# Routed rows split into bfloat16 parts during routing, and the branch for an expert's slots 65 to 96 put in front of its gate products

## The chip, the cores and the metric

The kernel runs on one core of a Trainium2 chip. The metric is device microseconds of one execution, as the median over runs. The engines are named as in the profile: PE (TensorE, matrix products; PEld is its weight load, which overlaps), DVE (VectorE), ACT (ScalarE), POOL (GpSimd) and SP, which here issues nearly all transfers. An engine name with a q (PEq, SPq) is that engine's instruction queue.

## The reference, cut to what matters

A sequence of 256 rows of width 1024 passes a mixer (a Fourier part and a gated delta rule in two directions, with a context of 256 rows ahead of it) and then a mixture of 32 experts, of which each row takes its best 4:

```python
def _moe(h, w_router, b_router, w_gate, b_gate, w_up, b_up, w_down, b_down):
    logits = (h @ w_router + b_router).astype(jnp.float32)
    top_v, top_i = lax.top_k(logits, TOP_K)          # 4 of 32
    gates = jax.nn.softmax(top_v, axis=-1)
    ...
        xb = h_pad[tok]
        a = jnp.minimum(xb @ w_gate[e] + b_gate[e], SWIGLU_LIMIT)
        u = jnp.clip(xb @ w_up[e] + b_up[e], -SWIGLU_LIMIT, SWIGLU_LIMIT)
        y = (a * jax.nn.sigmoid(SWIGLU_ALPHA * a) * (u + 1.0)) @ w_down[e] + b_down[e]
        return y * gate[:, None].astype(y.dtype)
```

Everything is float32. Each expert has three weights of 1024x1024, so the experts' weights are 384 MB, each byte of which is used once.

## The kernel before, in words

**First part.** The mixer and the routing stand in pieces that `ORDER` names (`X0`, `X1`: output projection, row norm, router logits and top 4 of rows 0 to 127 and of rows 128 to 255; `w`: the load of one more weight chunk of 1 MB). A scheduler may move instructions of these pieces.

**Chunks.** An expert is 12 chunks of 1 MB: 0 to 3 gate, 4 to 7 up, 8 to 11 down. They go through a ring of 18 places (`ROOMS`), in order; SP issues a chunk when the place's last reader, 18 chunks earlier, is done. 16 chunks are under way before the experts begin; `load_ahead` issues 12 per expert.

**Experts.** From there on the order on PE, ACT, DVE and SP is that of the code (`manual_schedule`). Each expert has 64 fixed slots (`MAIN`), and 32 more (65 to 96) behind a branch that is taken when its count of rows is over 64. On PE, per expert e: two bias rows (L1154), 16 gate products into `pg` (L1160), two bias rows and 16 up products into `pu`, the branch L1319 with `hidden32` (gather, gate and up products and transposes for slots 65 to 96), the gather of rows for a later expert (L1121, from the rows' three bfloat16 parts `h2s` by one-hot products), four transposes (L1179), for even e `add_rows` (L1238, slots back to rows) and for odd e `gates_turned` (L1149), 16 down products into `pd` (L1188), and the branch L1345 with `down32`. A branch that isn't taken is a jump over the instructions of its block. A float32 product counts as two passes with a weight load each in the trace, so 16 products are x32 there.

**First expert.** The rows `h2a` are made by DVE (L1050) after routing. Expert 0 gathers its rows in float32 (`gather32`, L1129), two blocks of 128 columns at a time, between its gate products. The split into `h2s` (`split_rows`: ACT L1272, L1276; DVE L1274, L1278) comes behind the up products, then the gather of expert 1's rows, then `down_bias` (the down bias of all experts times the rows' gates: L1285, L1292 on PE).

Of the kernel before, what the change touches and what calls it, by code (L numbers as in the profile page):

```python
# [21 lines left out]
T = 256  # L22
# [70 lines left out]
for _n, _w in (("c", 8), ("cc", 8), ("g1", 8), ("conv", 60), ("gout", 1), ("alog", 16), ("dtb", 16), ("br", 32)):  # L93
# [21 lines left out]
def body(ctx, tc, x, cx, sv, rows, cf, mk, w_mod, w_in, w_out, w_router, w_gate, b_gate, w_up, b_up,  # L115
# [827 lines left out]


    g2h = g2q = gatT = None

    def late_rows():
        nonlocal g2h, g2q, gatT
        late = natx[:, 2].rearrange("p a h d -> p (a h d)")
# [64 lines left out]
    def start_sums(a):  # L1014
        for g in range(2):
            nc.tensor.matmul(yacc[a][g], ident, xnat[:, a, 512 * g:512 * g + 512], start=True, stop=False,
                             skip_group_check=True)
        yield
# [9 lines left out]
             "Y0": start_sums(0), "Y1": start_sums(1)}  # L1028
# [33 lines left out]
    bdg = yz[:, 0]  # L1062
    nc.gpsimd.memset(bdg, 0.0)
    for g, hs in enumerate(halves):
        nc.scalar.dma_start(bdg[64 * g:64 * g + 32], b_down[:, 512 * g:512 * g + 512])
    strb = keep.tile([128, 128], BF, name="strb")
    nc.gpsimd.tensor_copy(strb, C("strict"))
    pr = bank("t", 3, 32)
    nc.tensor.matmul(pr[:, 0], strb, mkb[:, 0], start=True, stop=True)
    nc.tensor.matmul(pr[:, 1], onesb, mkb[:, 0], start=True, stop=False)  # L1070
    nc.tensor.matmul(pr[:, 1], strb, mkb[:, 1], start=False, stop=True)
    nc.tensor.matmul(pr[:, 2], onesb, mkb[:, 0], start=True, stop=False)
    nc.tensor.matmul(pr[:, 2], onesb, mkb[:, 1], start=False, stop=True)
    for a in range(2):
        nc.vector.scalar_tensor_tensor(rk[:, a], pr[:, a], 1.0, selm[:, a], op0=OP.add, op1=OP.mult)
    io1 = C("iota1")

# [7 lines left out]
    oh_ = [None, None]  # L1085
    oh_[0], oh_[1], oh32_, ohov2, gfr = carve("A", [128, 128, 128, 64, 256], 2)
    nc.scalar.dma_start(gfr[:4], rows[14:16].rearrange("a (b f) -> (a b) f", b=2))
    hT__ = carve("A", [512, 512], 2)
    *xg_, ha0, ha1, hao2 = carve("hT", [1024, 1024, 512, 512, 1024])
    hao, hso = hao2[:, :512], hao2[:, 512:]  # L1090
    hs_, hu_ = carve("vnc", [512, 512])
    *og_, ot0, ot1, ov_, ovg_, xov_, qr_ = carve("gm", [256, 256, 256, 256, 256, 256, 256, 8])
# [147 lines left out]
    oh32 = onehot(oh32_, 0, 1, 0, MAIN, F32)  # L1240
    xgs = {p: xg_[p % 2].rearrange("p (k s) -> p k s", k=8) for p in range(E // 2)}
    ots = [v.rearrange("p (a t) -> p a t", a=2) for v in (ot0, ot1)]
    ohs, ogs, vs = {}, {}, {}
    for a in range(2):
        lr = part("mm", 1960 + 32 * a, 32)
        nc.scalar.activation(lr, lg[:, a], AF.Exp, bias=top[a])
        sm = tail.tile([128, 1], F32, name="sm", bufs=2)
        nc.vector.scalar_tensor_tensor(gat[:, a], lr, 1.0, selm[:, a], op0=OP.mult, op1=OP.mult, accum_out=sm)
        nc.vector.reciprocal(sm, sm)
        nc.vector.tensor_scalar(gat[:, a], gat[:, a], sm, None, op0=OP.mult)  # L1250
    cnt = keep.tile([1, 33], I32, name="cnt")
    nc.vector.tensor_copy(cnt[:, :32], pr[0:1, 2])
    over = keep.tile([1, 33], F32, name="over")
    nc.vector.tensor_scalar(over[:, :32], pr[0:1, 2], -float(SLOTS), None, op0=OP.add)
    nc.vector.tensor_scalar(over[:, :EARLY], pr[0:1, 2, :EARLY], -float(MAIN), None, op0=OP.add)
    nc.vector.tensor_reduce(over[:, 32:], over[:, :32], AX.X, OP.max)
    nc.vector.tensor_scalar(cnt[:, 32:], over[:, 32:], 0.0, None, op0=OP.max)
    dump("rk", rk)
    dump("gat", gat)
    pctx.close()  # L1260
    if "stop" in dbg:
        return
    mps = ctx.enter_context(tc.tile_pool(name="mps", bufs=1, space=PSUM))

    engines = [ET.PE, ET.Activation, ET.DVE]

    def split_rows():

        rest = [xg_[1].rearrange("p (k q) -> p k q", k=8), hao2.rearrange("p (k q) -> p k q", k=8)]
        src = [h2a[:, a].rearrange("p (q k) -> p k q", k=8) for a in range(2)]  # L1270
        for a in range(2):
            nc.scalar.activation(h2s[:, 0, a], src[a], AF.Copy)  # L1272
        for a in range(2):
            nc.vector.tensor_tensor(rest[a], src[a], h2s[:, 0, a], OP.subtract)  # L1274
        for a in range(2):
            nc.scalar.activation(h2s[:, 1, a], rest[a], AF.Copy)  # L1276
        for a in range(2):
            nc.vector.tensor_tensor(h2s[:, 2, a], rest[a], h2s[:, 1, a], OP.subtract)  # L1278

    def down_bias():  # L1280
        nc.vector.scalar_tensor_tensor(bdg, bdg, 2.0, g2h, op0=OP.mult, op1=OP.mult)
        p = mps.tile([128, T], F32, name="m")
        for a in range(2):
            for hs in halves:
                nc.tensor.matmul(p[hs.start:hs.start + 32, 128 * a:128 * a + 128], gat[:, a], ident, start=True,  # L1285
                                 stop=True, tile_position=(0, hs.start))
        for hs in halves:
            q = slice(hs.start, hs.start + 32)
            nc.vector.tensor_copy(gatT[q], p[q])
        for a in range(2):  # L1290
# [3 lines left out]
        nc.gpsimd.memset(yz, 0.0)  # L1294

    with tc.manual_schedule(engines={ET.PE, ET.Activation, ET.DVE, ET.SP}):
        for e in range(E):
            pair, j = divmod(e, 2)
            w = weights_[e]
            xg = xgs[pair][:, :, MAIN * j:MAIN * j + MAIN]  # L1300
# [15 lines left out]
            if e == 0:  # L1316
                split_rows()
            if e >= EARLY:
                with tc.If(vs[e] > MAIN, preferred_fallthrough_block=False):  # L1319
                    hidden32(e, w)  # L1320
            load_ahead(8)
            up_part(pu_, a)
            if e == 0:
                gather(xgs[0][:, :, MAIN:], ohs[0][:, :, 1:], range(8))
            elif pair + 1 < E // 2:
                gather(xgs[pair + 1], ohs[pair + 1], range(4 * j, 4 * j + 4))
# [3 lines left out]
            if e == 0:  # L1330
                down_bias()
            elif j == 0:
                add_rows(ots[(pair - 1) % 2], yp)
            else:
                gates_turned(ogs[pair], ots[pair % 2])
# [6 lines left out]
            if e == 0:  # L1342
                gather(xgs[1], ohs[1], range(4))
# [13 lines left out]
    with tc.If(v > 0):  # L1357
        for e in range(E):
# [3 lines left out]
            def more(first):  # L1362
                with tc.If(v > first):
# [4 lines left out]
                    xg = xgs[0][:, :, :64]  # L1368
# [82 lines left out]
```

## Time and profile before

| | |
|---|---|
| median of 3 runs | 1321.13 us (1320.93 to 1324.38) |
| the profiled execution | 1323.06 us, its span 1321.0 us |
| PE busy | 1181.6 us, 89% of the span |
| DVE / ACT / POOL busy | 419.9 / 175.6 / 94.7 us |
| weights and other reads | 447.5 MB; 422 GB/s where the queue is never empty |

The profiled execution's own time is 2.06 us over its span. Busy shares are averages over stages; the mixer ends, and the first expert begins, near 332 us.

### The profile page before, as it was taken

What the parts mean: (1) busy time and instruction counts of PE and PEld (TensorE: products, weight loads), DVE (VectorE), ACT (ScalarE), POOL (GpSimd) and SP (SyncE); (2) the same over time, 40 slices, a digit from 0 to 9 for tenths busy, and PEclk for the clock granted to TensorE, in tenths of its full rate; (3) what the DMA queues carried; (4) which work ended last, traced back from release to release, by engine and by line L of the source; (5) the groups of instructions that cost most, each with busy time, mean ns of one, the idle gap of its engine ahead of it and who ended that gap; (6) DMA issues with size and microseconds to landing.
All of it is one profiled execution on the core that took longest, in us unless ns stands there. A gap on an engine that the chain in (4) does not pass through costs nothing. (4 is left out here: it accounts for less than half of the span.)

```text
span 1321.0 us, 17783 instructions
## 1 busy us (share of the span) xinstructions
PE 1181.6 (89%) x7337; PEld 551.8 (42%) x7337; DVE 419.9 (32%) x909; ACT 175.6 (13%) x324; POOL 94.7 (7%) x90
## 2 busy tenths in 40 slices
PE   6989998989898998999989997988898989998995
PEld 3767776755443333333333333323243333333332
DVE  2598887647421112221212121211212111211112
ACT  3265444111200000000000000000000000000001
POOL 1032337130000000000000000000000000000000
PEclk9999998989898999999999999999998989998998
DMA  9913345736659999799999999999999899999992
GB/s 329 314 46 117 113 147 162 293 129 260 252 202 425 413 421 423 290 422 422 423 420 421 423 422 421 422 422 423 421 423 424 359 421 418 422 421 422 422 421 92
DMA packets 96176, 450.56 MB, mean 341 GB/s; under 512 B 9236, under 2 KB 44440, under 8 KB 46888
## 3 DMA queue, kind: packets, MB, share of 16 engines
q1 hardware_dynamic: 95024, 446.79, 84.3%
q8 instruction: 105, 1.72, 0.5%
q10 hardware_dynamic: 1016, 1.80, 0.4%
q14 instruction: 31, 0.25, 0.1%
HBM read 447.51 MB, written 1.05 MB: 340 GB/s over the span
## 5 line engine op out<-in xcount | busy, mean ns | idle before, releaser
L1188 PE MATMUL pd<-w,scA 128*64 128x512 f32 x1024 | 229.5, 600 | 3.2 <-issue 1.3
L1160 PE MATMUL pu<-w,schT 128*64 128x512 f32 x1024 | 227.2, 593 | 4.2 <-DMA w<-in_w_up 4.1
L1160 PE MATMUL pg<-w,schT 128*64 128x512 f32 x1024 | 228.0, 596 | 0.8 <-DMA w<-in_w_gate 0.7
L1188 PEld LDWEIGHTS pd<-w,scA 128*64 128x64 f32 x1024 | 72.1, 138 | 149.6 <-issue 140.0
L1160 PEld LDWEIGHTS pu<-w,schT 128*64 128x64 f32 x1024 | 72.0, 137 | 148.3 <-issue 129.5
L1349 DVE TENSOR_TENSOR xnat<-pd,natx 64x512 f32<-64x512 f32 x64 | 44.1, 689 | 268.4 <-PE pd L1188 267.9
L1160 PEld LDWEIGHTS pg<-w,schT 128*64 128x64 f32 x1024 | 71.9, 137 | 133.0 <-issue 126.4
L1121 PE MATMUL m<-scA,h2s 128*128 128x128 bf16 (+2 forms) x864 | 56.3, 225 | 48.2 <-issue 26.8
L1167 ACT ACTIVATE scvnc<-schT 128x512 f32<-128x512 f32 x32 | 20.2, 630 | 577.0 <-DVE schT L1166 577.0
L1166 DVE TENSOR_SCALAR schT<-pg 128x512 f32<-128x512 f32 x32 | 22.1, 692 | 207.6 <-PE pg L1160 207.6
L1121 PEld LDWEIGHTS <-h2s 128*128 128x128 bf16 x864 | 50.2, 103 | 75.5 <-PEq L1319 41.6
L1238 PE MATMUL y<-xnat,scgm 128*128 128x512 f32 x144 | 70.3, 634 | 6.6 <-issue 3.4
L1172 DVE TENSOR_SCALAR scvnc<-pu 128x512 f32<-128x512 f32 x32 | 22.1, 692 | 151.9 <-PE pu L1160 151.6
L1414 POOL TENSOR_TENSOR schT<-scvnc,scA 128x512 f32<-128x512 f32 x1 | 1.3, 1288 | 944.0 <-ACT scvnc L1413 944.0
L1180 ACT ACTIVATE scA<-pg 128x512 f32<-128x512 f32 x32 | 19.1, 597 | 296.8 <-PE pg L1179 292.5
L504 PE MATMUL u<-hT,w 128*128 128x256 f32 x192 | 51.2, 400 | 0.0
L1238 PEld LDWEIGHTS y<-xnat,scgm 128*128 128x128 f32 x144 | 28.5, 209 | 37.6 <-issue 36.0
L1122 DVE COPY schT<-m 128x512 f32<-128x512 f32 x31 | 21.4, 692 | 67.7 <-PE m L1121 67.7
L504 PEld LDWEIGHTS u<-hT,w 128*128 128x128 f32 x192 | 34.2, 193 | 7.0 <-issue 2.9
L315 ACT ACTIVATE w<-w,cst 128x256 f32<-128x256 f32 x80 | 33.7, 501 | 14.1 <-DMA w<-in_w_mod 13.3
L316 POOL TENSOR_TENSOR w<-w 128x1024 f32<-128x1024 f32 x10 | 23.7, 2370 | 94.4 <-ACT w L315 78.7
L1168 DVE SCALAR_TENSOR_TENSOR scvnc<-scvnc,schT 128x512 f32<-128x512 f32 x32 | 22.2, 692 | 22.3 <-ACTq L1319 20.2
(358 smaller groups left out, 1103.8 us busy)
## 6 DMA issues: line engine op xcount, KB each, us to landing
w<-in_w_gate SPq DMA_DIRECT2D x128, 1024.0 KB, 19.8
w<-in_w_up SPq DMA_DIRECT2D x128, 1024.0 KB, 19.3
w<-in_w_down SPq DMA_DIRECT2D x128, 1024.0 KB, 19.8
w<-in_w_mod SPq DMA_DIRECT2D x24, 1024.0 KB, 10.8
w<-in_w_in SPq DMA_DIRECT2D x6, 1024.0 KB, 7.9
w<-in_w_out SPq DMA_DIRECT2D x4, 1024.0 KB, 6.4
wk<-in_w_in SPq DMA_DIRECT2D x2, 1024.0 KB, 12.3
wv<-in_w_in SPq DMA_DIRECT2D x2, 1024.0 KB, 12.2
```

Of the source, the lines that this page charges most:

```text
L315: nc.scalar.activation(w[:, k], w[:, k], AF.Copy, scale=sil[:, k, 0:1])
L316: nc.gpsimd.tensor_tensor(w[:, 0:4], w[:, 0:4], w[:, 4:8], OP.add)
L504: nc.tensor.matmul(p[:, c, :], w[c2][:, k, 128 * c:128 * c + 128], hT[:, k, 256 * n:256 * n + 256], start=(k == 0), stop=(k == 7))
L1121: nc.tensor.matmul(p[:, i], h2s[:, s, a, k], o[a], start=(s + a == 0), stop=(s + a == 3))
L1122: nc.vector.tensor_copy(dst[:, ks[0]:ks[-1] + 1], p)
L1160: nc.tensor.matmul(p[64 * g:64 * g + 64], xg[:, k], w[k // 2][:, k % 2, 512 * g:512 * g + 512], start=False, stop=(k == 7), skip_group_che ...
L1166: nc.vector.tensor_scalar(a, p, 7.0, None, op0=OP.min)
L1168: nc.vector.scalar_tensor_tensor(hs_, hs_, 1.0, a, op0=OP.add, op1=OP.mult)
L1172: nc.vector.tensor_scalar(hu_, p, 7.0, -7.0, op0=OP.min, op1=OP.max)
L1188: nc.tensor.matmul(p[64 * g:64 * g + 64], hT_[:, k, 64 * i:64 * i + 64], w[8 + 2 * i + k // 2][:, k % 2, 512 * g:512 * g + 512], start=(i ...
L1238: nc.tensor.matmul(yacc[a][g], ot[:, a, :], y[:, g, :], start=False, stop=False, skip_group_check=True)
L1349: nc.vector.tensor_tensor(yp[MAIN * j:MAIN * j + MAIN, g, :], p[hs], g2h[hs], OP.mult)
```

## The change

Four edits belong together. (1) Rows 0 to 127 are split into their bfloat16 parts in a new routing piece `S`; rows 128 to 255 right after their top 4 (ACT and DVE, in halves of 512 columns; POOL subtracts for rows 0 to 127). The first gather, `gather_first`, uses these parts: 48 bfloat16 products into one bank, then two copies. `split_rows` and `gather32` go. (2) The gates and counts that the later code needs (`gates_and_counts`) come behind expert 0's up products. (3) The branch with `hidden32` stands in front of an expert's gate products, no longer behind its up products. (4) `down_bias` comes in expert 3 instead of expert 0. Tiles move so that this fits (`qn`, `oh0_`, `bdg`).

```diff
+    def split_first():
+        ...
+        nc.vector.scalar_tensor_tensor(h2a[:, 0].rearrange("p (k q) -> p q k", k=8), nat_order(xgs[0]), st[:, 12:13],
+                                       nat_order(vec[:, 0]), op0=OP.mult, op1=OP.add)
+        rest = by_block(xgs[0])
+        nc.scalar.activation(h2s[:, 0, 0], by_block(h2a[:, 0]), AF.Copy)
+        nc.gpsimd.tensor_tensor(rest, by_block(h2a[:, 0]), h2s[:, 0, 0], OP.subtract)
+        nc.scalar.activation(h2s[:, 1, 0], rest, AF.Copy)
+        nc.gpsimd.tensor_tensor(h2s[:, 2, 0], rest, h2s[:, 1, 0], OP.subtract)
+    def gather_first(dst, oh):
+        p = mps.tile([128, 8, MAIN], F32, name="m")
+        for a in range(2):
+            for s in range(3):
+                for k in range(8):
+                    nc.tensor.matmul(p[:, k], h2s[:, s, a, k], oh[:, a, 0], start=(a + s + k == 0),
+                                     stop=(a + s == 3), skip_group_check=True)
+        for ks in (slice(0, 2), slice(2, 8)):
+            nc.vector.tensor_copy(dst[:, ks], p[:, ks])
...
+            if e >= EARLY:
+                with tc.If(vs[e] > MAIN, preferred_fallthrough_block=False):
+                    hidden32(e, w)
             pg_ = mps.tile([128, 512], F32, name="pg")
             bias_rows(e, pg_, bias[0])
             if e == 0:
-                for k in range(0, 8, 2):
-                    gather32(xg, oh32, k, ("m", "pd")[k // 2 % 2])
-                    if k >= 2:
-                        times(pg_, w[0:4], xg, (k - 2, k - 1))
-                ohs[0] = onehot(oh_[0], 0, 2, 0, MAIN)
-                times(pg_, w[0:4], xg, (6, 7))
-            else:
-                times(pg_, w[0:4], xg)
+                gather_first(xg, ohs[0])
+            times(pg_, w[0:4], xg)
...
             if e == 0:
-                split_rows()
-            if e >= EARLY:
-                with tc.If(vs[e] > MAIN, preferred_fallthrough_block=False):
-                    hidden32(e, w)
+                gates_and_counts()
...
-            if e == 0:
+            if e == 3:
                 down_bias()
```

Two places show how instructions move. The first is PE between the down products of one expert and the gate products of the next. Before, from the end of `down32` (L1238 is its `add_rows`) on, to the branch L1319:

```order
L1345 UNCONDITIONAL_BRANCH
L1154 LDWEIGHTS idb
L1154 MATMUL pg<-bgu,idb 64x512
L1154 LDWEIGHTS idb
L1154 MATMUL pg<-bgu,idb 64x512
L1160 MATMUL pg<-w,schT 64x512 x16
L1154 LDWEIGHTS idb
L1154 MATMUL pu<-bgu,idb 64x512
L1154 LDWEIGHTS idb
L1154 MATMUL pu<-bgu,idb 64x512
L1160 MATMUL pu<-w,schT 64x512 x16
L1319 COMPARE_AND_BRANCH
```

A full gate and up stage stands between the two branches. Now, from an expert's down products (L1185) on, where L1358 is the branch with `down32` (32 products L1224, four L1235) and L1321 the branch with the next expert's `hidden32`:

```order
L1185 MATMUL pd<-w,scA 64x512 x16
L1358 COMPARE_AND_BRANCH
L1358 UNCONDITIONAL_BRANCH
L1224 MATMUL m<-w,scgm 32x256 x32
L1235 MATMUL y_3010<-xnat,scgm 128x512
L1235 MATMUL y_3011<-xnat,scgm 128x512
L1235 MATMUL y_3012<-xnat,scgm 128x512
L1235 MATMUL y_3013<-xnat,scgm 128x512
L1358 UNCONDITIONAL_BRANCH
L1321 COMPARE_AND_BRANCH
L1321 UNCONDITIONAL_BRANCH
```

Where neither is taken, PE leaves the first block by a jump and lands on the next branch at once, with nothing between the two. The second place is DVE ahead of the first gate products. Before, between the top 4 of rows 128 to 255 and the first copies out of `gather32` (L1130):

```order
L1075 SCALAR_TENSOR_TENSOR rk<-t,mm 128x32 x2
L1110 TENSOR_TENSOR scA<-cfk,rk 128x64 x2
L1249 RECIPROCAL sm<-sm 128x1
L1252 CAST cnt<-t 1x32
L1250 TENSOR_SCALAR gat<-gat,sm 128x32
L1254 TENSOR_SCALAR over<-t 1x32
L1255 TENSOR_SCALAR over<-t 1x1
L1256 TENSOR_REDUCE over<-over 1x1
L1257 TENSOR_SCALAR cnt<-over 1x1
L1130 COPY schT<-m 128x2x64
```

Now the rows themselves (L1257), ranks, one-hots (L1104) and the two subtractions of the split stand there:

```order
L1257 SCALAR_TENSOR_TENSOR natx<-xg,st,vec 128x64x8 x2
L1261 SCALAR_TENSOR_TENSOR rk<-u,mm 128x32 x2
L1104 TENSOR_TENSOR scgm<-cfk,rk 128x128 x2
L1264 TENSOR_TENSOR vec<-natx,h2s 128x8x64 x2
L1267 TENSOR_TENSOR h2s<-vec,h2s 128x8x64 x2
L1268 CAST cnt<-u 1x32
L1269 TENSOR_SCALAR over<-u 1x32
L1270 TENSOR_SCALAR over<-u 1x1
L1127 COPY schT<-m 128x2x64
L1127 COPY schT<-m 128x6x64
```

The gates have left this place, and the split of rows 128 to 255 has come into it.

## Rows read from the trace of the kernel before

**Rows 1.** The page: DMA kinds, costliest groups (busy, mean ns, idle before, releaser)

```profile
q8 instruction: 105, 1.72, 0.5%
...
L1160 PE MATMUL pu<-w,schT 128*64 128x512 f32 x1024 | 227.2, 593 | 4.2 <-DMA w<-in_w_up 4.1
...
L1166 DVE TENSOR_SCALAR schT<-pg 128x512 f32<-128x512 f32 x32 | 22.1, 692 | 207.6 <-PE pg L1160 207.6
```

**Rows 2.** Stretches: us, PE, PEld, DVE, ACT, POOL busy, PEclk, DMA share, GB/s

```profile
380.00:390.00 10.00, 10.00 (x52) 3.28 (x50) 1.39 (x2) 0.63 (x1) 0.00 (x0) 1.00 0.29 120
...
540.00:550.00 10.00, 10.00 (x50) 3.36 (x48) 1.38 (x2) 0.63 (x1) 0.00 (x0) 1.00 0.34 143
...
570.00:580.00 10.00, 10.00 (x48) 3.04 (x44) 1.38 (x2) 0.63 (x1) 0.00 (x0) 1.00 1.01 422
```

**Rows 3.** Timeline of PE, experts 7 and 8: start, length, what [idle before]

```profile
565.67 0.41 PE L1154 MATMUL pg<-bgu,idb 96*64 96x512 bf16 x2 [0.55 <-PEq L1345]
...
591.29 0.41 PE L1154 MATMUL pg<-bgu,idb 96*64 96x512 bf16 x2 [0.64 <-PEq L1345]
...
619.25 0.41 PE L1154 MATMUL pg<-bgu,idb 96*64 96x512 bf16 x2 [0.45 <-PEq L1345]
```

**Rows 4.** Timeline of PE, expert 5, which takes both branches

```profile
504.90 1.36 PE L1121 MATMUL m<-scA,h2s 128*128 128x32 bf16 x48
...
506.99 7.05 PE L1207 MATMUL m<-w,scgm 128*32 128x512 f32 x64
...
529.22 3.66 PE L1227 MATMUL m<-w,scgm 128*32 128x256 f32 x64
```

**Rows 5.** Timeline of PE, waits of over 1 us ended by issue

```profile
417.62 0.72 PE L1121 MATMUL m<-scA,h2s 128*128 128x128 bf16 x10 [0.66 <-PEq L1319]
423.01 1.67 PE L1121 MATMUL m<-scA,h2s 128*128 128x128 bf16 x14 [4.67 <-issue]
...
665.29 0.47 PE L1121 MATMUL m<-scA,h2s 128*128 128x128 bf16 x4 [4.23 <-issue]
...
753.28 6.23 PE L1188 MATMUL pd<-w,scA 128*64 128x512 f32 x27 [1.30 <-issue]
...
809.37 1.97 PE L1121 MATMUL m<-scA,h2s 128*128 128x128 bf16 x17 [4.85 <-issue]
...
900.01 5.29 PE L1238 MATMUL y<-xnat,scgm 128*128 128x512 f32 x8 [3.44 <-issue]
...
958.76 2.51 PE L1121 MATMUL m<-scA,h2s 128*128 128x128 bf16 x24 [4.19 <-issue]
...
1069.76 0.91 PE L1121 MATMUL m<-scA,h2s 128*128 128x128 bf16 x7 [4.01 <-issue]
...
1209.28 1.65 PE L1121 MATMUL m<-scA,h2s 128*128 128x128 bf16 x14 [4.84 <-issue]
```

**Rows 6.** Timeline of PE, start and end of expert 2

```profile
402.60 0.41 PE L1154 MATMUL pg<-bgu,idb 96*64 96x512 bf16 x2 [0.64 <-PEq L1345]
...
437.10 0.41 PE L1154 MATMUL pg<-bgu,idb 96*64 96x512 bf16 x2 [0.55 <-PEq L1345]
```

**Rows 7.** A stretch behind the first of these waits, columns as in group 2

```profile
423.00:427.00 4.00, 3.99 (x21) 3.19 (x22) 1.09 (x3) 0.60 (x1) 0.00 (x0) 0.56 1.01 424
```

**Rows 8.** Timeline of PE behind the last expert, at the branch L1357

```profile
1308.40 1.09 PE L1404 MATMUL m<-scA,cfk 4*128 4x256 f32 x4 [1.66 <-PEq L1357]
```

**Rows 9.** Timeline of PE, expert 0 and what ends it

```profile
330.99 0.18 PE L1071 MATMUL t<-mkb,strb 128*128 128x32 bf16 x1 [2.55 <-DVE mkb L941]
...
362.92 1.07 PE L1285 MATMUL m<-cfk,gat 128*32 128x128 f32 x8
...
368.62 7.09 PE L1188 MATMUL pd<-w,scA 128*64 128x512 f32 x32
...
377.08 0.41 PE L1154 MATMUL pg<-bgu,idb 96*64 96x512 bf16 x2
```

**Rows 10.** Who waited for whom, SP's queue: us in total, times, longest

```profile
SPq L982 <- PEq L1319: 168.7, 21, 18.8
```

More of the change, by code (lines that the diff above doesn't have):

```diff
@@ L948, in late_rows @@
         nonlocal g2h, g2q, gatT
-        late = natx[:, 2].rearrange("p a h d -> p (a h d)")
+        late = qn.rearrange("p a h d -> p (a h d)")
         g2h, g2q, gatT = late[:, :512], late[:, 512:768], late[:, 768:]
@@ L1061, in body @@
     yp, yz = xnat[:, 0].rearrange("p (g f) -> p g f", g=2), xnat[:, 1].rearrange("p (g f) -> p g f", g=2)
[L1062 to L1065, printed above, removed]
     strb = keep.tile([128, 128], BF, name="strb")
     nc.gpsimd.tensor_copy(strb, C("strict"))
[L1068 to L1075, printed above, removed]
     io1 = C("iota1")
+    nc.gpsimd.memset(yz, 0.0)
     def carve(tag, widths, bufs=1):
@@ L1083, in carve @@
         return [t[:, int(i):int(j)] for i, j in zip(o, o[1:])]
[L1085 to L1092, printed above, removed]
+    *og_, ot0, ot1, ov_, ovg_, xov_, qr_, oh0_ = carve("gm", [256, 256, 256, 256, 256, 256, 256, 8, 128])
     ov = ov_.rearrange("p (k s) -> p k s", k=4)
@@ L1238, in add_rows @@
                 nc.tensor.matmul(yacc[a][g], ot[:, a, :], y[:, g, :], start=False, stop=False, skip_group_check=True)
-    oh32 = onehot(oh32_, 0, 1, 0, MAIN, F32)
-    xgs = {p: xg_[p % 2].rearrange("p (k s) -> p k s", k=8) for p in range(E // 2)}
-    ots = [v.rearrange("p (a t) -> p a t", a=2) for v in (ot0, ot1)]
     ohs, ogs, vs = {}, {}, {}
[L1244 to L1250, printed above, removed]
@@ L1259, in body @@
-    dump("gat", gat)
+    oh_ = [oh0_, None]
+    engines = [ET.PE, ET.Activation, ET.DVE]
+    hand = tc.manual_schedule(engines={ET.PE, ET.Activation, ET.DVE, ET.SP, ET.Pool})
+    with hand:
+        hv, rest = by_block(h2a[:, 1]), by_block(vec[:, 2])
+        hi, mid, lo = h2s[:, 0, 1], h2s[:, 1, 1], h2s[:, 2, 1]
+        kh = (slice(0, 64), slice(64, 128))
+        next(parts["X1"])
+        pr = bank("u", 3, 32)
+        nc.tensor.matmul(pr[:, 0], strb, mkb[:, 0], start=True, stop=True)
+        nc.tensor.matmul(pr[:, 1], onesb, mkb[:, 0], start=True, stop=False)
+        nc.tensor.matmul(pr[:, 1], strb, mkb[:, 1], start=False, stop=True)
+        nc.tensor.matmul(pr[:, 2], onesb, mkb[:, 0], start=True, stop=False)
+        nc.tensor.matmul(pr[:, 2], onesb, mkb[:, 1], start=False, stop=True)
+        for i in range(2):
+            fs = slice(512 * i, 512 * i + 512)
+            nc.vector.scalar_tensor_tensor(hv[:, :, kh[i]].rearrange("p k q -> p q k"), nat_order(xgs[1][:, fs]),
+                                           st[:, 13:14], nat_order(vec[:, 0, fs]), op0=OP.mult, op1=OP.add)
+            nc.scalar.activation(hi[:, :, kh[i]], hv[:, :, kh[i]], AF.Copy)
+        for a in range(2):
+            nc.vector.scalar_tensor_tensor(rk[:, a], pr[:, a], 1.0, selm[:, a], op0=OP.add, op1=OP.mult)
+        ohs[0] = onehot(oh_[0], 0, 2, 0, MAIN)
+        for q in kh:
+            nc.vector.tensor_tensor(rest[:, :, q], hv[:, :, q], hi[:, :, q], OP.subtract)
+            nc.scalar.activation(mid[:, :, q], rest[:, :, q], AF.Copy)
+        for q in kh:
+            nc.vector.tensor_tensor(lo[:, :, q], rest[:, :, q], mid[:, :, q], OP.subtract)
+        nc.vector.tensor_copy(cnt[:, :32], pr[0:1, 2])
+        nc.vector.tensor_scalar(over[:, :32], pr[0:1, 2], -float(SLOTS), None, op0=OP.add)
+        nc.vector.tensor_scalar(over[:, :EARLY], pr[0:1, 2, :EARLY], -float(MAIN), None, op0=OP.add)
@@ L1262, in body, with gates_and_counts @@
         return
+    oh_[1], ohov2, gfr = carve("A", [128, 64, 256], 2)
+    hT__ = carve("A", [512, 512], 2)
+    *xg_, ha0, ha1, hao2 = carve("hT", [1024, 1024, 512, 512, 1024])
+    hao, hso = hao2[:, :512], hao2[:, 512:]
+    hs_, hu_ = carve("vnc", [512, 512])
+    xgs_ = {p: xg_[p % 2].rearrange("p (k s) -> p k s", k=8) for p in range(E // 2)}
+    ots = [v.rearrange("p (a t) -> p a t", a=2) for v in (ot0, ot1)]
+    bdg = h2a[:, 0, :512]
     mps = ctx.enter_context(tc.tile_pool(name="mps", bufs=1, space=PSUM))
[L1265 to L1270, printed above, removed]
+    def gates_and_counts():
         for a in range(2):
[L1272 to L1278, printed above, removed]
+            lr = part("mm", 1960 + 32 * a, 32)
+            nc.scalar.activation(lr, lg[:, a], AF.Exp, bias=top[a])
+            sm = tail.tile([128, 1], F32, name="sm", bufs=2)
+            nc.vector.scalar_tensor_tensor(gat[:, a], lr, 1.0, selm[:, a], op0=OP.mult, op1=OP.mult, accum_out=sm)
+            nc.vector.reciprocal(sm, sm)
+            nc.vector.tensor_scalar(gat[:, a], gat[:, a], sm, None, op0=OP.mult)
+        nc.vector.tensor_reduce(over[:, 32:], over[:, :32], AX.X, OP.max)
+        nc.vector.tensor_scalar(cnt[:, 32:], over[:, 32:], 0.0, None, op0=OP.max)
+        nc.scalar.dma_start(gfr[:4], rows[14:16].rearrange("a (b f) -> (a b) f", b=2))
+        nc.gpsimd.memset(bdg, 0.0)
+        for g in range(2):
+            nc.gpsimd.dma_start(bdg[64 * g:64 * g + 32], b_down[:, 512 * g:512 * g + 512])
     def down_bias():
@@ L1293, in down_bias @@
                                  skip_group_check=True)
-        nc.gpsimd.memset(yz, 0.0)
-    with tc.manual_schedule(engines={ET.PE, ET.Activation, ET.DVE, ET.SP}):
+    with tc.manual_schedule(engines={ET.PE, ET.Activation, ET.DVE, ET.SP, ET.Pool}):
         for e in range(E):
@@ L1323, in body @@
             if e == 0:
-                gather(xgs[0][:, :, MAIN:], ohs[0][:, :, 1:], range(8))
+                gather(xgs_[0][:, :, MAIN:], ohs[0][:, :, 1:], range(8))
             elif pair + 1 < E // 2:
-                gather(xgs[pair + 1], ohs[pair + 1], range(4 * j, 4 * j + 4))
+                gather(xgs_[pair + 1], ohs[pair + 1], range(4 * j, 4 * j + 4))
             if e + 1 < E:
@@ L1329, in body @@
             hT_ = turned(a)
-            if e == 0:
+            if e == 3:
                 down_bias()
-            elif j == 0:
+            if j == 0 and e:
                 add_rows(ots[(pair - 1) % 2], yp)
-            else:
+            elif j:
                 gates_turned(ogs[pair], ots[pair % 2])
@@ L1342, in body @@
             if e == 0:
-                gather(xgs[1], ohs[1], range(4))
+                gather(xgs_[1], ohs[1], range(4))
             if e >= EARLY:
```

36 lines of the change are left out of this document (13 added, 23 removed), and 2 rows, old and new, of the table ORDER.

## Prediction

> **What bounds the kernel now.** I read the page first, then the stretches, then PE's timeline expert by expert. At 422 GB/s, a full stream, a chunk of 1 MB takes 1,048,576 / 422,000 = 2.49 us and an expert's 12 chunks 29.8 us [rows 2]. PE takes 25.6 us for an odd expert and 28.0 us for an even one, 26.8 us in the mean [rows 3]. So PE is the faster of the two in the steady state, and one would look for its waits in the weights. They are hardly there: the up products, the costliest of such groups, waited 4.1 us for weights in the whole execution [rows 1]. Instead the stream stands still at places, at 29% and 34% of its rate near 385 and 545 us, with PE busy all the while [rows 2]: the ring is full and PE is late. PE begins late (expert 0), loses about 20 us in each of the two experts that take their branches, and loses time in one more way, which I think decides this change.
>
> That way is seen in [rows 5]: seven times PE stands still for 3.44 to 4.85 us, and once for 1.30 us, "issue" (no semaphore, no data), each a few microseconds behind a branch L1319 that wasn't taken. Counted through the built order (a bfloat16 product is one load and one pass, a float32 one two of each), the seven are 5392, 3337, 2053, 1285, 2054 and 3338 instructions apart: 21.06, 13.04, 8.02, 5.02, 8.02 and 13.04 times 256. Instructions arrive in 105 packets, 1.72 MB, 16.4 KB each [rows 1], and PE's order to the end of the last expert is 104 times 256 long. So PE's instructions come in blocks of 256, and these are waits for a block. When do they occur? The jump over `hidden32` is 250 instructions long (of its 244 products and loads, 48 gather products and 64 passes in [rows 4], each with a load, are 224), so it nearly always lands in the next block. In all eight cases the block after that one begins 2 to 76 instructions behind the landing. In the other jumps over `hidden32` it begins 81 or more behind, and none waits. The jump over `down32` is 149 long (64 passes with loads [rows 4], and the adds). Where it stays within its block, the boundary has come as near as 7 instructions behind it, without a wait. I read this as: PE holds the block it is in and the next one; the one after is asked for on entry and comes some 5.4 us after the jump (417.62 to 423.01 [rows 5]).
>
> [...]
>
> **What each wait costs.** Expert 2 took 34.50 us [rows 6] for 27.96 [rows 3]: 6.5 us for a wait of 4.67. [...] The eight waits sum to 31.5 us, with seven times 1.9 us they cost 45 us.
>
> **The change part by part.**
>
> *The branch moved.* Now the jump over `down32` and that over the next expert's `hidden32` follow each other with one branch between. Together they are about 411 instructions, over a block and a half. Laid against the 256 grid that the seven waits fix (my count runs ahead of it by 2 per expert, taken out), this pair crosses two boundaries ahead of experts 2, 3, 8, 10, 11, 13, 15, 16, 18, 23, 24, 26, 28, 29 and 31, fifteen times (ahead of 5 and 21 too, but there the second branch is taken). [...] The wait is new in kind and not in the trace: from below, a jump to a far block with no stream running took 1.66 us at the end of the kernel [rows 8]; from above 5.4 us as in [rows 5]. The stream still runs, so I take a value near the upper row: wait and clock as measured for such a wait, 6.5 us each, 15 x 6.5 = 97 us. In experts 6, 9, 14, 19 and 27 one boundary is crossed and the next lies 10, 44, 30, 4 and 24 instructions behind the landing. There gate products run at 7.09 / 64 = 0.11 us per instruction (32 passes and 32 loads, as for the down products in [rows 9]), so 5.4 us less this way is 4.3, 0.6, 2.1, 5.0 and 2.8 us; with the clock about 20 us. The old eight vanish with their place: minus 45 us.
>
> The gap of 0.66 us between up products and gather [rows 5] goes; the transposes behind that gather wait for DVE's two steps of 0.69 us [rows 1] anyway, so 0.4 us of it counts. A second branch at the down products adds perhaps 0.2 us. Net minus 0.2 x 31 = 6 us; bounds 0 and minus 12.
>
> *Earlier release.* SP waited 168.7 us at the branch L1319 [rows 10], since `hidden32` was the last reader of gate and up chunks, taken or not. Now a gate place is free when the gate products are done. That lets the stream run further ahead; it gives PE only the 4 us that it waited. For the two experts that take the branch all eight chunks must be there before `hidden32`; the stream is then some 20 us ahead, so I cost it at nothing (without that lead, up to 10 us each).
>
> *The first expert.* From the ranks' products at 330.99 to expert 1's bias at 377.08 it takes 46.1 us [rows 9]. Now DVE has, behind the top 4 (about 330): two halves of the rows, ranks and one-hots (0.9 us), four halves of subtractions, at 0.69 us per half [rows 1] 5.0 us in all; ACT's halves and POOL's lie beside these. Eight products and a copy later the gate products begin, near 335.8. Then 7.1 gate, 7.1 up, 7.1 down [rows 9], two gathers of 48 and 24 products (1.9 and 1.5 us, an estimate from 10 products in 0.72 us [rows 5]), 1.4 for transposes and copy with nothing beside them, 0.6 branch: expert 1 begins near 362.5, 14.5 us earlier. `down_bias`, 362.92 to 368.62 = 5.7 us on PE [rows 9], comes back in expert 3, before the stream has caught up with PE, so moving it wins nothing. Net minus 8.5 us. Expert 1's chunks that wait for the gates' work (about 347) land by 357 and are needed from 370.
>
> *Sum*, against the profiled execution's own 1323.06 us: minus 8.5 (start), minus 4 (weights), minus 45 (old waits), minus 6 (gaps), plus 97 and 20 (new waits): 1376.6. That execution is 1.9 us above the median of its runs, so I predict 1374 us, 4% slower. With 3.5 to 7.3 us per wait it is 1330 to 1392.
>
> **The rivals.**
>
> *A jump pair costs no more than a jump.* Then PE's instructions are held further ahead than I read, or the fetch overlaps the drain. With waits as many as before the time is 1323 - 8.5 - 4 - 6 - 1.9 = 1303 us; with none at all the stream decides: filled from 347 us on, the last 366 chunks end at 347 + 366 x 2.49 = 1258, and with the last products and the final norm about 1280. For it: 62 branches stood in the kernel and only eight led to a wait. Against it: those eight stand on the grid, and no deeper store would let them arise. Chance 0.17.
>
> *Short fetches.* Once PE is slower than 29.8 us per expert, the ring is full, the stream has pauses and a block may come sooner, towards the 1.66 us of [rows 8]. It decides at one price: 15 waits and the 20 us scaled with them balance 8.5 + 4 + 45 + 6 = 63.5 us at 3.5 us per wait, clock included. At 3 us the time is about 1312. Against it: with 26.6 + 4 us per expert the stream still runs at 97%. Chance 0.13, of which 0.04 within 0.3%.
>
> *The change's own aim.* Start and earlier release shift the whole stream forward, and PE follows it. That needs PE to wait for weights now, which 4.1 us do not bear out; it is in the first rival's lower end.
>
> **How the numbers follow.** My forecast has 0.70. 0.3% (4 us) is about what a measurement of this kernel can tell from no change. Slower by more 0.70, within 0.04, faster 0.26 (0.17 and 0.09). The range reaches down to the first rival, 1300, and up to the upper bound, 1392; what it leaves out is the stream's 1280 and a dearer wait.
>
> **What would show it.** Right: waits of 3 us and more ended by PE's queue or issue at the fifteen places named, ahead of the bias rows, none behind the up products; the clock below full behind each; even and odd experts without a wait 0 to 0.4 us shorter; expert 1 near 362; SP's long waits at gate and up products and no longer at a branch; the stream never short. Wrong: gaps of 1 us or less at all pairs of branches, or PE waiting for weights over many experts.

## The result and the profile after

The changed kernel takes **1387.84 us** (median of 4 runs, 1386.80 to 1389.63) where the kernel before takes 1321.03 us on the same chip: a ratio of 1.0507 (95% interval 1.0478 to 1.0537), 5% slower. 1374 us, slower, was predicted, with a range of 1300 to 1392. The profiled execution took 1387.12 us, its span is 1385.0 us, 64.0 us more than before.

What PE waits for, from the view of the waits of the changed kernel (us in total, times, longest; L1151 are the bias rows, L1157 the gate and up products, L1321 the branch with `hidden32`):

```profile
PE pg L1151 <- issue: 76.4, 15, 6.5
PE pg L1151 <- PEq L1321: 14.3, 14, 1.2
PE pg L1157 <- issue: 13.7, 5, 4.6
```

Fifteen waits ended by issue stand ahead of an expert's first bias row, and five inside the gate products. Before there were eight, of 31.5 us together, behind the up products [rows 5]. Four of the fifteen and one of the five, from PE's timeline (experts 2, 3, 11, 31; the third row is expert 6):

```profile
398.27 0.64 PE L1151 MATMUL pg<-bgu,idb 96*64 96x512 bf16 x2 [6.44 <-issue]
434.09 0.64 PE L1151 MATMUL pg<-bgu,idb 96*64 96x512 bf16 x2 [6.46 <-issue]
...
548.62 8.73 PE L1157 MATMUL pg<-w,schT 128*64 128x512 f32 x29 [4.58 <-issue]
...
705.44 0.41 PE L1151 MATMUL pg<-bgu,idb 96*64 96x512 bf16 x2 [4.25 <-issue]
...
1340.72 0.41 PE L1151 MATMUL pg<-bgu,idb 96*64 96x512 bf16 x2 [3.59 <-issue]
```

Assigned to experts, the fifteen are 2, 3, 8, 10, 11, 13, 15, 16, 18, 23, 24, 26, 28, 29 and 31: each that was named, and no other. None is left behind the up products. The costliest groups of the page (busy, mean ns, idle before):

```profile
L1157 PE MATMUL pg<-w,schT 128*64 128x512 f32 x1024 | 269.2, 678 | 14.2 <-issue 13.7
L1185 PE MATMUL pd<-w,scA 128*64 128x512 f32 x1024 | 226.8, 595 | 6.9 <-ACT scA L1177 6.2
L1157 PE MATMUL pu<-w,schT 128*64 128x512 f32 x1024 | 228.0, 592 | 0.0
...
L1151 PE MATMUL pg<-bgu,idb 96*64 96x512 bf16 x64 | 15.2, 471 | 95.9 <-issue 76.4
```

The up products now wait for nothing, where they waited 4.2 us [rows 1]. The gate products, which come right behind the waits, take 678 ns each, the up and down products 592 and 595. Stretches of the same trace show why: the first two lie right behind waits (of 6.44 and 3.94 us), the third lies within expert 0, 7.5 us after PE began it.

```profile
398.27:402.27 4.00, 4.00 (x12) 1.31 (x14) 0.00 (x0) 0.00 (x0) 0.00 (x0) 0.50 1.02 424
828.69:832.69 4.00, 4.00 (x12) 1.18 (x14) 0.00 (x0) 0.00 (x0) 0.00 (x0) 0.59 1.01 420
...
344.00:348.00 4.00, 4.00 (x22) 1.37 (x20) 0.14 (x1) 0.00 (x0) 0.00 (x0) 1.00 0.00 0
```

The granted clock (third number from the end) is 0.50 in the first, 0.59 in the second and 1.00 in the third; over the 4 us behind each of the fifteen waits it is 0.50 to 0.66. SP's queue has lost its wait at the branch with `hidden32` [rows 10]; it now waits where a place of the ring is freed. The wait at the other branch has grown (L1358 is the branch with `down32`; before it was L1345, the first row):

```profile
SPq L982 <- PEq L1345: 54.5, 13, 9.3
...
SPq L1001 <- PEq L1358: 289.2, 27, 12.9
SPq L1001 <- PE pg L1157: 287.6, 116, 17.6
SPq L1001 <- PE pu L1157: 149.6, 111, 1.5
```

So the earlier release of the chunks took place, and the chunks came early enough that PE waited for none. It bought the 4 us, and no more, because PE was the slower of the two.

### The profile page after: what moved, and what is told of

It is laid out like the page before. It is cut to its first block, busy times and chain, and to the rows that moved or that the text cites. A ratio compares the mean times of both kernels' runs of the same rounds, so it can differ in the third digit from the quotient of the medians.

```text
span 1385.0 us, 17933 instructions
## 1 busy us (share of the span) xinstructions
PE 1199.1 (87%) x7353; PEld 552.3 (40%) x7353; DVE 422.5 (31%) x906; ACT 172.9 (12%) x326; POOL 99.8 (7%) x94
## 3 DMA queue, kind: packets, MB, share of 16 engines
HBM read 447.51 MB, written 1.05 MB: 324 GB/s over the span
## 5 line engine op out<-in xcount | busy, mean ns | idle before, releaser
L1157 PE MATMUL pg<-w,schT 128*64 128x512 f32 x1024 | 269.2, 678 | 14.2 <-issue 13.7
L1185 PE MATMUL pd<-w,scA 128*64 128x512 f32 x1024 | 226.8, 595 | 6.9 <-ACT scA L1177 6.2
L1157 PE MATMUL pu<-w,schT 128*64 128x512 f32 x1024 | 228.0, 592 | 0.0
L1157 PEld LDWEIGHTS pg<-w,schT 128*64 128x64 f32 x1024 | 83.9, 156 | 179.6 <-issue 177.3
L1157 PEld LDWEIGHTS pu<-w,schT 128*64 128x64 f32 x1024 | 77.3, 137 | 137.7 <-issue 134.6
L1185 PEld LDWEIGHTS pd<-w,scA 128*64 128x64 f32 x1024 | 70.7, 137 | 150.1 <-issue 139.1
L1362 DVE TENSOR_TENSOR xnat<-pd,qn 64x512 f32<-64x512 f32 x64 | 44.1, 688 | 264.8 <-PE pd L1185 264.3
L1151 PE MATMUL pg<-bgu,idb 96*64 96x512 bf16 x64 | 15.2, 471 | 95.9 <-issue 76.4
L1235 PE MATMUL y<-xnat,scgm 128*128 128x512 f32 x144 | 65.1, 595 | 2.8 <-DVE xnat L1229 1.9
L1151 PEld LDWEIGHTS <-idb 96*64 96x64 bf16 x128 | 7.8, 111 | 129.2 <-issue 123.7
L1115 PEld LDWEIGHTS <-h2s 128*128 128x128 bf16 x864 | 44.4, 98 | 31.1 <-issue 25.5
L1235 PEld LDWEIGHTS y<-xnat,scgm 128*128 128x128 f32 x144 | 26.0, 191 | 30.7 <-issue 26.1
L1115 PE MATMUL m<-scA,h2s 128*128 128x128 bf16 (+1 forms) x480 | 27.3, 211 | 4.0 <-DVE scgm L1102 3.8
```

What stands on the lines that cost most here:

```text
L1115: nc.tensor.matmul(p[:, i], h2s[:, s, a, k], o[a], start=(s + a == 0), stop=(s + a == 3))
L1151: nc.tensor.matmul(p[64 * g:64 * g + 64], idb[:, e:e + 1].to_broadcast([96, 64]), b[:, 512 * g:512 * g + 512], start=True, stop=False, ski ...
L1157: nc.tensor.matmul(p[64 * g:64 * g + 64], xg[:, k], w[k // 2][:, k % 2, 512 * g:512 * g + 512], start=False, stop=(k == 7), skip_group_che ...
L1185: nc.tensor.matmul(p[64 * g:64 * g + 64], hT_[:, k, 64 * i:64 * i + 64], w[8 + 2 * i + k // 2][:, k % 2, 512 * g:512 * g + 512], start=(i ...
L1235: nc.tensor.matmul(yacc[a][g], ot[:, a, :], y[:, g, :], start=False, stop=False, skip_group_check=True)
L1362: nc.vector.tensor_tensor(yp[MAIN * j:MAIN * j + MAIN, g, :], p[hs], g2h[hs], OP.mult)
```

## The experiments

Seven kernels ask where the waits come from: each changes what lies between the two jumps, where the jumps stand against the blocks, or what else the transfers do. An eighth asks about the down bias, three more about the start.

**The branch back behind the up products**, all else as changed:

```diff
+            if e >= EARLY:
+                with tc.If(vs[e] > MAIN, preferred_fallthrough_block=False):
+                    hidden32(e, w)
             load_ahead(8)
```

> The changed kernel with the branch of hidden32 put back behind the up products; start, split and late down bias stay. Theory 1 (waits for instruction blocks at jump pairs): all fifteen waits ahead of the bias rows vanish; the jump over hidden32 alone leaves six or seven waits again, in the gather behind it, at experts 2, 10, 13, 18, 23 and 28 (8, 15 and 26 on the edge). About 1304 us (1295 to 1312), so some 17 us below the kernel before. Rival (the new start and split cost the time, not the branch): stays near 1388 us.

Measured: 1317.18 us, ratio 0.9953 (0.9933 to 0.9972). The 70 us are gone, so the place of the branch is their cause. But 17 us less than before were expected, and 6 came. The trace has seven waits, not six:

```profile
752.03 0.39 PE L1176 MATMUL pg<-cfk,schT 128*128 128x128 f32 x2 [3.83 <-issue]
...
958.75 2.72 PE L1115 MATMUL m<-scA,h2s 128*128 128x128 bf16 x24 [6.26 <-issue]
```

The wait of expert 13 grew from 1.30 us [rows 5] to 3.83, and that of expert 20, which was to go, stayed, at 6.26 us. All seven sum to 32.4 us, where the eight before came to 31.5. What is left is the start, of which more below: by the traces it gives 3.5 us (expert 1 comes 7.0 us sooner behind the first product of the ranks, and the down bias takes 3.5 us in expert 3); the rest of the 6 us wasn't followed.

**The branch alone moved**, in the kernel before:

```diff
+            if e >= EARLY:
+                with tc.If(vs[e] > MAIN, preferred_fallthrough_block=False):
+                    hidden32(e, w)
             pg_ = mps.tile([128, 512], F32, name="pg")
```

> The kernel before with one edit: the branch of hidden32 in front of the gate products. Theory 1: waits of 3.5 to 6.5 us ahead of the bias rows of experts 2, 3, 7, 8, 10, 13, 15, 16, 18, 20, 23, 24, 26, 28, 29 and 31 (sixteen), none behind the up products; about 1397 us, 1385 to 1410. Rival (the new start): stays near 1321 us.

Measured: 1393.89 us, ratio 1.0531 (1.0490 to 1.0572). All sixteen waits stand ahead of the experts named, and no seventeenth. The branch alone does all of the harm.

**Branches only where they are taken.** `if e >= EARLY` becomes `if e in (5, 21)` at both branches; slots over 64 of other experts, of which these inputs have none, are left out:

> The changed kernel with both branches kept only for experts 5 and 21, which take them with these inputs; the other experts have no branch, so that slots over 64 would be lost there with other inputs. Theory 1: no wait for instructions is left, PE runs ahead and waits for weights, and the stream sets the end: 1278 to 1290 us. Rival (the order of hidden32's pass costs the time): 1350 us and more, since the two experts that run it keep their order.

Measured: 1293.69 us, ratio 0.9786 (0.9757 to 0.9816), 94 us under the changed kernel. No wait for issue is left on PE in the experts; it waits for weights instead, and the stream is full (view of the waits, then a stretch):

```profile
PE pu L1157 <- DMA w<-in_w_up: 25.9, 52, 1.6
PE pg L1157 <- DMA w<-in_w_gate: 8.6, 17, 0.7
...
600.00:900.00 300.00, 275.84 (x1394) 96.94 (x1390) 55.10 (x94) 14.27 (x26) 0.00 (x0) 1.00 1.01 423
```

With the jumps away the stream decides, at 4 us more than the upper end expected. 94 us is what 58 jumps over code that isn't run cost beyond that.

**One jump at a time**: the branch with `down32` only for experts 5 and 21 (which leaves out slots over 64 of the others' down products), that with `hidden32` for all, ahead of the gate products:

> The changed kernel with the branch of down32 kept only for experts 5 and 21 (others would lose slots over 64 with other inputs); the branch of hidden32 stays in front of the gate products in all. Theory 1: a jump of 250 lands in a block that is there, so no wait stands ahead of the bias rows; waits of 1 to 5 us come inside the gate products where the next block begins less than 49 instructions on. 1295 to 1330 us. Rival (the place in front of the gate products costs, pair or not): 1370 us and more, waits ahead of the bias rows.

Measured: 1315.12 us, ratio 0.9947 (0.9929 to 0.9966). No wait ahead of a bias row; eight of over 1 us inside gate products (experts 3, 12 to 14, 23 to 26), the largest

```profile
1140.07 8.03 PE L1157 MATMUL pg<-w,schT 128*64 128x512 f32 x30 [5.52 <-issue]
```

That is 21 us above the version without the jumps, where the pair costs 94. It is the pair that makes the kernel slower, not the place ahead of the gate products.

**The branch between the gate part and the up products**, so that a gate or an up stage stands between any two jumps:

```diff
             a = gate_part(pg_)
+            if e >= EARLY:
+                with tc.If(vs[e] > MAIN, preferred_fallthrough_block=False):
+                    hidden32(e, w)
             pu_ = mps.tile([128, 512], F32, name="pu")
```

> The changed kernel with the branch of hidden32 between gate and up products: the two jumps are apart, and behind the landing stand float32 products of 0.11 us per instruction in place of the gather's quick ones. Theory 1: waits only where the next block begins less than 49 instructions behind the landing, experts 7, 12, 17, 25 and 30, 1 to 4 us each; 1283 to 1297 us, below the version with the branch behind the up products. Rival (any place in front of the up products costs): 1340 us and more.

Measured: 1305.06 us, ratio 0.9868 (0.9837 to 0.9900). This version leaves nothing out and beats both kernels. Its waits are five, at the experts named (7, 12, 17, 25, 30), of 1.13 to 4.30 us; the largest:

```profile
850.10 8.09 PE L1157 MATMUL pu<-w,schT 128*64 128x512 f32 x29 [4.30 <-issue]
```

It stands 11.4 us above the version without the jumps, and its waits sum to 10.7 us. The expectation missed by 8 us, as that for the version without jumps missed by 4.

**The blocks shifted**: 60 small products, whose result nobody reads, stand ahead of expert 0, 120 instructions with their loads:

```diff
+        pad = bank("t", 3, 32)
+        for i in range(60):
+            nc.tensor.matmul(pad[:, i % 3], (strb, onesb)[i % 2], mkb[:, 0], start=True, stop=True)
```

> The changed kernel with 60 small products (120 instructions on PE, into an unused bank) ahead of the first expert, while PE waits for the split: it computes the same. Theory 1 (block grid of 256 instructions): the experts with a wait of 3.5 us and more ahead of their bias rows change to 3, 4, 7, 9, 11, 12, 14, 17, 19, 20, 24, 25, 27 and 30; experts 2, 8, 10, 13, 16, 18, 23, 26, 28, 29 and 31 lose theirs. Time as the changed kernel, within 12 us. Rival (what stands at these experts, their data or their transfers, causes the waits): the same experts as without the shift.

Measured: 1391.82 us, ratio 1.0533 (1.0496 to 1.0570). All fourteen named experts wait, and one more (15, with 2.34 us). Expert 2, first of the fifteen, has lost its wait ahead of the bias rows (1.17 us are left there, the jumps themselves) and waits for 1.00 us inside its gate products; expert 4, which was free, waits as long as any:

```profile
430.07 0.64 PE L1151 MATMUL pg<-bgu,idb 96*64 96x512 bf16 x2 [6.18 <-issue]
466.78 0.64 PE L1151 MATMUL pg<-bgu,idb 96*64 96x512 bf16 x2 [6.47 <-issue]
```

(these are experts 3 and 4). Nothing in an expert's own code or data was touched, so what decides is where the jumps stand in the order, counted in blocks of 256.

**No stream**: the first 18 chunks are used by all experts, nothing is loaded behind them, so the products are of other weights than the reference's:

```diff
+        if nchunk[0] >= NW:
+            nchunk[0] += 1
+            return held[(nchunk[0] - 1) % NW]
```

> The changed kernel with the weights of the first 18 chunks used again by all later experts: nothing is loaded after them, and the output is that of the wrong weights. Theory 1 with fetches that queue beside the stream: some fifteen waits stay ahead of bias rows but shrink to 1.3 to 2.5 us each; time 1290 to 1325 us. If the fetch time doesn't depend on the stream: 4 to 6 us each, 1370 us and more. Rival (PE waits for weights there): none is left, near 1265 us.

Measured, in a single run: 1351.92 us, between what the two theories gave. Fifteen waits again, at the same experts but for 20 in place of 24, each of 3.58 to 4.21 us, with the transfers idle (the waits, and a stretch over the first):

```profile
PE pg L1155 <- issue: 58.2, 15, 4.2
...
394.00:398.00 4.00, 0.22 (x4) 0.01 (x2) 1.38 (x2) 0.00 (x0) 0.00 (x0) 1.00 0.02 4
```

A wait of this kind takes 3.9 us in the mean with no other weight transfer at all. In the changed kernel the fifteen fall in two kinds. Two of either kind as stretches, each from the start of the wait to its end:

```profile
1244.92:1248.96 4.04, 0.00 (x1) 0.00 (x2) 1.38 (x2) 0.00 (x0) 0.00 (x0) 1.00 0.73 243
1337.13:1340.72 3.59, 0.00 (x0) 0.00 (x0) 1.38 (x2) 0.00 (x0) 0.00 (x0) 1.00 0.02 5
391.83:398.27 6.44, 0.00 (x2) 0.01 (x2) 1.38 (x2) 0.00 (x0) 0.00 (x0) 0.82 1.02 422
1176.28:1182.69 6.41, 0.01 (x1) 0.00 (x1) 1.38 (x2) 0.00 (x0) 0.00 (x0) 0.87 1.02 424
```

Eight last 3.59 to 4.33 us, with transfers at 0.96 of their rate or below; seven last 5.75 to 6.46 us, with transfers at 1.01 or 1.02. The seven last 6.28 us in the mean, the eight 4.06; beside these and the 3.9 us of the run without a stream, I estimate that a full stream adds about 2.3 us to such a wait. The two kinds are not so clean everywhere: in the version with the branch alone moved, expert 23's wait lasted 5.08 us at a share of 0.76, and expert 28's 4.99 us at 1.01.

**The down bias back in expert 0**:

> The changed kernel with the down bias back in expert 0. Theory 1: PE does the same work in all, and PE is never ahead of the stream before expert 5: the same time within 4 us. Rival (moving it off the start won its 5.7 us): 1393 us.

Measured: 1392.12 us, ratio 1.0526 (1.0493 to 1.0558); the changed kernel's is 1.0507 (1.0478 to 1.0537). The intervals overlap, so the two expectations aren't told apart. Its waits of over 1 us for issue are at the same experts, and two more in experts 1 (3.83 us) and 9 (1.05 us, 0.79 in the changed kernel). The down bias itself takes 3.5 us in either place (359.78 to 363.29 here).

The last three ask about the start. In the changed kernel the first products of expert 0 wait for the last steps of routing, and two tiny steps of DVE (start, length) are ten times as long as their like:

```profile
324.76 2.06 DVE L142 TENSOR_TENSOR rst<-rsr 128x1 f32<-128x1 f32 x1
...
328.32 2.44 DVE L941 TENSOR_TENSOR mm<-mm 128x32 f32<-128x32 f32 x1
```

Each ends where one of POOL's two new subtractions ends, 324.68 + 2.12 = 326.80 and 328.57 + 2.13 = 330.70:

```profile
324.68 2.12 POOL L958 TENSOR_TENSOR xg<-natx,h2s 128x1024 f32<-128x1024 f32 x1 [1.09 <-ACT h2s L957]
...
328.57 2.13 POOL L960 TENSOR_TENSOR h2s<-xg,h2s 128x1024 bf16<-128x1024 f32 x1
```

**The version with the branch in the middle once more**, on the same chip as the next two:

> The version with the branch between gate part and up products once more, to stand beside the next two on one chip: 1305 us within 3, five waits in front of up products at experts 7, 12, 17, 25 and 30, and 41.9 us from the first rank product to expert 1's first bias row.

Measured: 1305.04 us, ratio 0.9884 (0.9838 to 0.9929), the five waits, 41.5 us from the first rank product to expert 1.

**The two subtractions on DVE**, in that version (`nc.gpsimd.tensor_tensor` becomes `nc.vector.tensor_tensor`, twice):

> The version with the branch between gate part and up products, and the two subtractions of the new routing piece on DVE instead of POOL. Theory: in the changed kernel DVE's step L142 on 128x1 took 2.06 us for its usual 0.15, and L941 on 128x32 took 2.44 for 0.19, each ending with one of POOL's two subtractions of 2.1 us, because POOL holds DVE up: some 4.2 us on the way to the ranks. With the subtractions on DVE these two rows are 0.15 and 0.19 us, DVE works 2 x 1.3 us more, and the products of the ranks wait 3 to 4.5 us for mkb in place of 5.55: expert 1 is 1 to 2.5 us nearer to the first rank product, the time 1 to 3 us below that of the version it is made from. Rival: the long rows have to do with DVE's own work there, they stay, and the start is 2.6 us later: 1 to 4 us above.

Measured: 1302.39 us, ratio 0.9852 (0.9809 to 0.9895). Both rows are back at their length, and the rank products wait 2.1 us less for DVE:

```profile
328.57 0.15 DVE L142 TENSOR_TENSOR rst<-rsr 128x1 f32<-128x1 f32 x1
...
331.24 0.19 DVE L941 TENSOR_TENSOR mm<-mm 128x32 f32<-128x32 f32 x1
...
331.70 0.19 PE L1252 MATMUL u<-mkb,strb 128*128 128x32 bf16 x1 [3.43 <-DVE mkb L942]
```

Expert 1 comes 38.6 us behind the first rank product in place of 41.5, and the time is 2.65 us less, though in single runs the two versions overlap. Only two waits for issue of over 1 us are left, at experts 7 and 25, and all such waits sum to 6.0 us in place of 10.6; why the others went wasn't followed. So the 2.65 us can't be put down to the start alone: start and waits together are 7.5 us less, of which PE gives back 3.1 us in waits for weights (7.7 us in place of 4.6).

**POOL's two subtractions left out**: the second and third part of rows 0 to 127 are zeros written by ACT:

> The same version with POOL's two subtractions left out: the second and third part of rows 0 to 127 are zeros that ACT writes, so the products see these rows in bfloat16 alone. Theory: L142 back at 0.15 us and L941 at 0.19 us, the ranks' products wait about 1.3 us for mkb in place of 5.55, and 37 to 38.5 us lie between the first rank product and expert 1's first bias row, in place of 41.9. The time is then about 1301 us (1297 to 1305 in one look). Rival: POOL has nothing to do with it, both rows stay at 2 us and more, and the stretch at 41 to 42 us.

Measured, in a single run: 1301.58 us; L142 and L941 at 0.16 and 0.19 us, a wait of 1.69 us, 38.0 us to expert 1. Both rows are back as soon as POOL's two steps are gone, whether DVE does their work or nobody does: POOL's steps are the cause.

## Why the prediction was right, and where it was short

**The reading held.** That PE holds a block of 256 instructions and the next one, so that a pair of jumps that passes two boundaries has to wait, is my reading; no view shows which blocks PE holds. What the runs show agrees with it in three ways: the fifteen experts named from the count alone are the fifteen that wait, for 3.59 to 6.46 us; the shift of 120 instructions moved the waits to the fourteen experts that the same count gave, and to one more; and keeping one jump of the pair ended the waits ahead of the bias rows.

**The terms**, predicted and read from the traces, with the span as the whole:

| term | predicted | read | from |
|---|---|---|---|
| old waits and their clock | -45 | -48.3 | 31.5 us of waits; 16.8 us less busy time in gathers, transposes, down products and `add_rows` |
| new waits and their clock | +117 | +133.3 | 76.4 + 13.7 us of waits; gate products 41.2 us longer, their bias rows 2.0 |
| gaps at branches and behind them | -6 | -7.9 | idle of PE in gathers, transposes, bias rows and down products from expert 1 on |
| weights | -4 | -4.9 | the gate and up products' waits, now none |
| start | -8.5 | -6.3 | expert 1 at 367.31 in place of 377.08, and 3.5 us for the down bias later; 3.0 us of it lie ahead of the first product of the ranks |
| sum | 53.5 | 65.9 | the span grew by 64.0 |

The forecast was short above all by the size of **"6.5 us each"**. A wait ahead of bias rows was 76.4 / 15 = 5.1 us, not 4.67; the loss behind it was sized about right, 2.0 us for 1.9 (the gate products of those fifteen experts took 28.2 us more than 7.04 each, their bias rows 2.0). The 1.9 us are what expert 2 took longer, 34.50 - 27.96 [rows 6, 3], less its wait of 4.67; no row gives the clock's part of them, only the 0.56 granted behind that wait [rows 7], and behind the fifteen it was 0.50 to 0.66. Wait and loss together were 7.1 us. That 4.67 came so near the mean is in part luck: seven waits lasted 6.28 us in the mean and eight, beside a pausing stream, 4.06. The prediction took the one price for both. I read the longer ones so: the old waits, from which the price was taken, begin some instructions behind a landing, and these begin with it. The old rows bear this out: from the end of the up products (417.62 - 0.66 = 416.96) to the end of the wait (423.01) it is 6.05 us [rows 5], as long as a new wait beside a full stream. The five inside the gate products were forecast at 4.3, 0.6, 2.1, 5.0 and 2.8 us and came as 4.58, 0.79, 3.18, 2.32 and 2.80: 13.7 us for 14.8. The gate products there took 10.8 us longer, where 5 were left for the clock; over the 4 us behind the wait it was 0.50 in experts 6, 19 and 27 and 1.00 in 9 and 14. The gate products of experts 5, 21 and 22, of which two run `hidden32` first, took 4.3 us more, which stood in no term.

The two ends of the range are not of one sum: with 3.5 us per wait the prediction's terms give 1330 if the 20 us stay as they are; with 7.3 us they give 1387 so, and 1390 with the 20 us scaled; 1392 leaves out the 1.9 us. Two of its signs did not come. SP's long waits at a branch did not go, they moved to the branch with `down32`. And the second branch takes more than "perhaps 0.2 us", which no row gave: where a pair has no such wait, PE idles for 1.06 to 1.18 us, and at one branch L1345 alone it idled for 0.43 to 0.67 us.

**The start** was mis-sized by more, in proportion. It has to be counted from the first product of the ranks, since the mixer's end differs by 4 us between runs of the same code up to there (325.27 to 329.65 us); in the two profiled executions it lies at 325.27 and 328.24 (the first two rows are of the kernel after, the third of before, the last two the down bias after and what follows it):

```profile
325.27 0.18 PE L1250 MATMUL u<-mkb,strb 128*128 128x32 bf16 x1
331.03 0.18 PE L1252 MATMUL u<-mkb,strb 128*128 128x32 bf16 x1 [5.56 <-DVE mkb L942]
...
328.24 0.18 PE L1069 MATMUL t<-mkb,strb 128*128 128x32 bf16 x1
...
452.10 0.63 PE L1305 MATMUL m<-cfk,gat 128*32 128x128 f32 x8
...
455.61 0.44 PE L1146 MATMUL m<-cfk,scgm 128*128 128x128 f32 x2
```

From there to expert 1 it is 42.04 us, before 48.84: 6.8 us less, where 14.5 were forecast. The down bias takes 3.5 us back and not 5.7, so 3.3 us are left of 8.5. That expert 1, put at 362.5, came at 367.31 and no later is luck: the mixer had ended 3.0 us sooner.

Two steps failed. The first is that "POOL's lie beside these": POOL's subtractions held DVE up by 1.9 and 2.25 us on the way to the ranks, as the last two experiments show, and PE waited there for 5.56 us in place of 2.55 [rows 9]. By what means isn't shown. The first held-up step lies beside POOL's row from start to end (324.76 to 326.82, POOL's 324.68 to 326.80). The second agrees in its end alone (330.76, POOL's 330.70): it starts at 328.32, 0.25 us ahead of POOL's row, and 0.19 us would have been enough; what held it until then isn't shown either. The second step is "eight products and a copy later the gate products begin": the bias rows now wait for the counts (`over`), which come last on DVE, at 336.41 (forecast near 335), so all 48 products of the first gather come behind them, at a granted clock of 0.50 (336 to 340 us):

```profile
336.47 0.64 PE L1151 MATMUL pg<-bgu,idb 96*64 96x512 bf16 x2 [5.19 <-DVE over L1270]
337.04 2.74 PE L1124 MATMUL m<-scgm,h2s 128*128 128x64 bf16 x48
340.17 7.64 PE L1157 MATMUL pg<-w,schT 128*64 128x512 f32 x32 [0.38 <-DVE schT L1127]
...
367.31 0.41 PE L1151 MATMUL pg<-bgu,idb 96*64 96x512 bf16 x2 [0.57 <-PEq L1321]
```

The gate products were put at 335.8 and begin at 340.17: that is 4.3 of the 7.7 us that are missing, and 3.0 are PE's longer wait for the ranks.

**The rivals.** That a pair costs no more than a jump is refuted by the one-jump and the middle version, which pay single jumps alone. Short fetches were to decide at 3.5 us per wait, clock included; without any stream a wait is 3.9 us in the mean, 3.58 at the least, before the loss behind it, so a pause of the stream would not have reached that. What was right in it is that the wait is shorter where the stream pauses, 4.06 us in the mean for 6.28, and that eight of the fifteen were of this kind. The change's own aim, chunks released earlier, is there in SP's waits, and pays only once PE is fast enough to need it: without the jumps PE waits 34.5 us for weights.

## What to carry to other kernels

Here branches that weren't taken were not free: 58 jumps, over blocks of 149 and 250 instructions, cost 94 us. Count the engine's instructions, and where two jumps with little between pass two boundaries of 256 instructions, as the waits here fix them, put a stage of work between them (here 1388 to 1305 us by moving one branch). Price such a wait by waits that begin at a landing (here 6.28 us in the mean beside the full stream, 4.06 beside a pausing one), and add what is lost behind it (here 2.0 us, at a granted clock of 0.50 to 0.66). Before work goes to an idle engine, ask which steps of a neighbour overlap it: POOL's two subtractions, 2.12 and 2.13 us long, held DVE up for 1.9 and 2.25 us.

## What the runs showed of the hardware that was not expected

A wait at a pair of jumps took 3.58 to 4.21 us with the transfers idle (the run without a stream), and 5.75 to 6.46 us beside the full stream of the changed kernel. Behind its waits of 4 us and of 6.5 us alike the granted clock was 0.50 to 0.66 over the next 4 us, and the gate products and bias rows there took 2.0 us longer per wait. Not every wait for issue has this behind it: after one of 3.18 us (expert 14) the clock stayed at 1.00, and so it did after one of 3.96 us in the version with the branch alone moved (expert 3):

```profile
438.32:442.32 4.00, 4.00 (x20) 1.43 (x22) 0.00 (x0) 0.00 (x0) 0.00 (x0) 1.00 1.01 420
```

A DVE step on 128x1 elements took 2.06 us in place of 0.15, and one on 128x32 took 2.44 in place of 0.19, beside a POOL subtraction of 2.1 us.
